# Three 16-bit products per dense token in the expert layer, narrower 32-bit products, and one set of h rows spread eight blocks later

## The chip, the core and the metric

The kernel runs on one core of one Trainium2 chip. The metric is device microseconds (us) of one execution, lower is better: 2103.4 us is the median of 3 runs, which lie between 2100.66 and 2104.29 us. The trace is of one execution, taken by the hardware profiler. PE is the TensorE matmul, PEld its weight load, DVE the VectorE, ACT the ScalarE, POOL the GpSimd engine, SP the engine that issues the large loads.

## The reference, cut to what matters

Two blocks run on 256 tokens of width 1024. The first has two layers, each with a convolution branch, a causal attention of 8 heads with values of 64 wide, and a gated branch of 4 heads of 64. The second has two mixers and behind each an expert layer, which is where most of the time goes:

```
q = (h @ w_q).reshape(B, S, 8, 2, 128)
scores = einsum('bshpd,hpkd->bshpk', q, sub_keys)        # 2 x 128 keys per head
s1, i1 = top_k(scores[..., 0, :], 16); s2, i2 = top_k(scores[..., 1, :], 16)
cand = s1[..., :, None] + s2[..., None, :]               # 256 sums per head
top_s, top_pos = top_k(cand, 16)
ids  = take(i1 * 128 + i2, top_pos)                      # 16 of 16384 experts
gate = softmax(top_s)
act  = gelu(einsum('thk,td->thk over d', u_tab[ids], h)) # u and v rows of the experts
out  = einsum('thk,thkd->td', gate * act, v_tab[ids])
```

A token has 8 heads x 16 = 128 slots; each slot has a gate and an expert, named by two keys below 128.

## The kernel before, in words

Nearly all data and products are 32-bit. The first layers, the mixers and the head of the expert layer are ordered by a scheduler; the body of the expert layer stands in a block whose order is written by hand (`tc.manual_schedule()`), so that each engine's instructions stand as the loop issues them. Each engine works its own list in that order, and an instruction that waits holds up those behind it.

**The expert layer (`peer`, called twice).** The first TS = 96 tokens are done by gathers: an indirect DMA (`fetch`) brings the u row and later the v row of slot k, one row per partition, and `own(k)` works on it in one DVE instruction (L1323 for u, L1332 for v). Their h rows are needed spread over partitions, 32 tokens at a time: `own_rows(r)` copies columns of hT with ACT (L1294, L1295) into a tile of the 12-deep ring "r", turns them on PE (L1299), and ACT writes them to one half of "hh" (L1300).

The other TD = 160 tokens are dense: the kernel multiplies them with all 16384 experts. In the u stage the loop goes over 128 blocks of 128 experts. In block j `u_mm` (L1353) multiplies a block of u with hT, 8 products of 160 columns, and `u_act` of block j-1 applies gelu on ACT and writes W (L1360, L1363). W[:, j, t] must also be multiplied with the gate of expert and token, zero for nearly all. That is spread in groups g of 4 tokens, one group every second block from j = 40 on, 40 groups:

- `hot(g)`: DVE compares the two keys of each slot with 0..127 (L1370), two one-hot matrices per token; ACT multiplies the second with the gates (L1373, 4 instructions).
- `meet(g)`, two blocks later: PE multiplies the two matrices of each token over the 128 slots (L1380), which gives its 128 x 128 grid of gates.
- `put(g)`, two blocks later again: DVE multiplies the grid into the blocks of W that are done (L1388), ACT copies it into those that aren't (L1390), where `u_act` then multiplies (L1364).

After block 127 the v stage (L1452) multiplies W with v, block by block.

The slots of the second 128 tokens are turned into columns by `slot_columns` at j = 39 (L1184, L1188), with rows that DVE makes at j = 29 and 34 (L1175, L1154). `own_rows(1)` stands at j = 37, `own_rows(2)` at j = 72. The ring "r" holds the gathered rows, the one-hot matrices and the tiles of `own_rows`.

**The first layers.** Sums of squares come from products with a matrix of ones, 128 columns of which one is read (L510). In `values` each head's product with v (L726 to L728) takes the v of two neighbouring heads, 128 columns, and half of the result is used; in `sgu` (L822) it is the same with the gated rows.

Of the kernel before, what the change touches and what calls it, by code (L numbers as in the profile page):

```python
# [137 lines left out]
class Kernel:  # L138
# [322 lines left out]
    def first_layer(self, l):  # L461
        nc, tc = self.nc, self.tc
        W = lambda u: self.w3(f"win{l}", u * SLOT)
        with tc.tile_pool(name=f"l{l}", bufs=1) as pl, tc.tile_pool(name=f"m{l}", bufs=2) as pm:
# [9 lines left out]
            with tc.tile_pool(name=f"a{l}", bufs=1) as pa:  # L474
# [17 lines left out]
                for g in range(4):  # L492
                    if g == 1:
                        with self.behind():
                            w = W(g)
                    else:
                        w = W(g) if g else first
                    ps = self.proj3_T(w)
                    self.ada(ADA[l][0][g])
                    sq = self.t(pm, (P, 2, S), "sq")  # L500
                    nc.scalar.activation(sq, ps, AF.Square)
                    for a in range(2):
                        f = 2 * g + a
                        gain = self.col("q_norm_g", f, l) if f < 6 else self.col("kv_norm_g", f - 6, l)
                        if a:
                            nc.vector.tensor_scalar(cT[:, f], ps[:, a], gain, None, op0=ALU.mult)
                        else:
                            nc.scalar.activation(cT[:, f], ps[:, a], AF.Copy, scale=gain)
                        for b in range(2):
                            nc.tensor.matmul(pss[:, (0 if f < 6 else 2) + b], sq[:, a, b * P:(b + 1) * P],  # L510
                                             self.ones[:, :P], start=f == 0 and b == 0, stop=f == 7 and b == 1,
                                             skip_group_check=True)
# [198 lines left out]
    def values(self, pm, sc, rl, v, y):  # L711
        nc = self.nc

        po = [[self.acc.tile([P, 4, P], F32, name="acc") for _ in range(2)] for _ in range(2)]
        for h in range(8):
# [8 lines left out]
            vv = [v[:, b, h - h % 2:h - h % 2 + 2].rearrange("p a d -> p (a d)") for b in range(2)]  # L724
            o = [po[b][h // 4][:, h % 4] for b in range(2)]
# [3 lines left out]
        for b in range(2):  # L729
            yv = y[:, b, 256:768].rearrange("p (h d) -> p h d", h=8)  # L730
            for g in range(2):
                for e in range(2):
                    hs = slice(4 * g + e, 4 * g + 4, 2)
                    nc.vector.tensor_tensor(yv[:, hs], po[b][g][:, e::2, e * 64:(e + 1) * 64],
                                            rl[:, hs, b:b + 1].to_broadcast([P, 2, 64]), op=ALU.mult)
# [59 lines left out]
    def sgu(self, l, pl, pm, wm, wuv):  # L795
# [22 lines left out]
        def mix(y):  # L818
            for b in range(2):
                ps = self.psum((P, 4, P))  # L820
                for h in range(4):
                    nc.tensor.matmul(ps[:, h], ws[:, h], gs[b][:, (h // 2) * P:(h // 2 + 1) * P], start=True, stop=True)  # L822
                for h in range(4):
                    nc.vector.scalar_tensor_tensor(y[:, b, 768 + h * 64:768 + (h + 1) * 64],
                                                   ps[:, h, (h % 2) * 64:(h % 2 + 1) * 64],
# [366 lines left out]
    def peer(self, l):  # L1192
# [9 lines left out]
        with ExitStack() as ctx:  # L1202
# [63 lines left out]
            accs = [lr[:, k * D:(k + 1) * D] for k in (1, 0)]  # L1266

# [67 lines left out]
            with tc.manual_schedule():  # L1335
# [30 lines left out]

                def hot(g):
                    o = self.rp.tile([P, 2, 4, P], F32, name="r")
                    k = TS + 4 * g
                    nc.vector.tensor_tensor(o, self.iota[:, None, None].to_broadcast([P, 2, 4, P]),  # L1370
                                            slots[:, 1:3, k:k + 4, None].to_broadcast([P, 2, 4, P]), op=ALU.is_equal)
                    for t in range(4):
                        nc.scalar.activation(o[:, 1, t], o[:, 1, t], AF.Copy, scale=slots[:, 0, k + t:k + t + 1])  # L1373
                    one[g] = o

                def meet(g):
                    o = one.pop(g)
                    ps = self.acc.tile([P, 4, P], F32, name="acc")
                    for t in range(4):
                        nc.tensor.matmul(ps[:, t], o[:, 0, t], o[:, 1, t], start=True, stop=True)  # L1380
# [16 lines left out]
                for j in range(P):  # L1397
# [21 lines left out]
                    if j == 39:  # L1419
                        self.slot_columns(1, *late, slots)  # L1420
                        c1.close()
                        wts["b"] = self.t(pool("pw"), (P, P - JW, TD), "Wb")
                    if j in (37, 72):
                        own_rows(1 if j == 37 else 2)
# [105 lines left out]
```

## Time and profile before

| | |
|---|---|
| median of 3 runs | 2103.4 us (2100.66 to 2104.29) |
| profiled execution: its own time, its span in the trace | 2102.61 us, 2100.9 us |
| u stage of the expert layer, first and second (window) | 661 to 996, 1469 to 1804 us |
| v stage, first and second (window) | 996 to 1285, 1804 to 2088 us |
| TensorE granted clock, mean | 0.979 of full speed |

The time is 1.7 us above the span; the rest of the text counts in the span and adds that. A matmul in 32 bits leaves two records per product in the trace, one in 16 bits leaves one, and a record's duration is longer than the distance to the next, since they are pipelined: what one costs is read from the distance between starts of runs of them. The same holds for DVE and ACT in short: an instruction of 1.22 us can be followed 1.14 us after its start. An idle time that the profile shows in brackets ends with the engine named behind the arrow.

### The profile page before, as it was taken

The page shows a single profiled execution, that of the slowest core. Times are in us where ns is not written, and L with a number is a line of the kernel's source. Part 1 is how long each engine was busy: PE and PEld are TensorE (multiplying, and loading weights), DVE is VectorE, ACT ScalarE, POOL GpSimd, SP SyncE. Part 2 cuts the span into 40 slices and gives each one's busy share as a digit, 9 for nine tenths or more (in the row PEclk, how much of TensorE's full clock was granted, in tenths as well). Part 3 has the DMA queues.
Part 4 walks back from the last instruction along what each step waited for, and adds up shares of the span by engine and source line. Part 5 has one row for each costly group of instructions (what it writes and reads, how often), then busy time and mean ns, then how long its engine had stood idle before and what let it go on. Part 6 is the DMA issues. An engine that isn't in the chain of part 4 may idle for free. (4 is left out here: it accounts for less than half of the span.)

```text
span 2100.9 us, 35398 instructions
## 1 busy us (share of the span) xinstructions
PE 1998.1 (95%) x13860; PEld 1871.6 (89%) x13860; DVE 1403.3 (67%) x3068; ACT 617.7 (29%) x1684; POOL 626.3 (30%) x683
## 2 busy tenths in 40 slices
PE   6997998999999989999999998999989999999997
PEld 6683795888769989999999998969989999999997
DVE  7698588577657777788444446976796788544344
ACT  4452472455433134433000002743224433000000
POOL 0201111011001564443343440001374444243442
PEclk9998999999999999999999998999999999999999
DMA  9647738442414999999999998643799999999996
GB/s 343 233 160 265 262 111 310 149 123 71 161 61 157 356 405 364 358 365 363 381 415 416 415 415 338 243 180 120 294 404 377 353 366 372 356 416 416 415 415 270
DMA packets 123719, 630.01 MB, mean 300 GB/s; under 512 B 13728, under 2 KB 14368, under 8 KB 79264
## 3 DMA queue, kind: packets, MB, share of 16 engines
q1 hardware_dynamic: 66960, 422.87, 52.5%
q0 software_dynamic: 55296, 201.35, 24.6%
q10 hardware_dynamic: 1296, 3.53, 0.5%
q8 instruction: 109, 1.79, 0.3%
q14 instruction: 58, 0.48, 0.1%
HBM read 626.65 MB, written 1.05 MB: 299 GB/s over the span
## 5 line engine op out<-in xcount | busy, mean ns | idle before, releaser
L1353 PE MATMUL ps<-hT,w 128*128 128x160 f32 x4096 | 574.8, 300 | 0.0
L1353 PEld LDWEIGHTS ps<-hT,w 128*128 128x128 f32 x4096 | 562.4, 191 | 0.0
L1332 DVE SCALAR_TENSOR_TENSOR hl<-r,asl,hl 128x1024 f32<-128x1024 f32 x186 | 239.0, 1285 | 314.8 <-DMA r<-v,ids 314.2
L1452 PE MATMUL acc<-Wa,w 128*128 128x160 f32 x2560 | 348.4, 299 | 0.0
L1452 PEld LDWEIGHTS acc<-Wa,w 128*128 128x128 f32 x2560 | 347.9, 190 | 0.0
L1311 POOL DMA_INDIRECT r<-v,ids x192 | 232.0, 1208 | 346.4 <-PE acc L1452 255.1
L1311 POOL DMA_INDIRECT r<-urow,ids x192 | 252.7, 1316 | 243.3 <-DVE r L1323 133.6
L1323 DVE SCALAR_TENSOR_TENSOR r<-r,hh 128x1024 f32<-128x1024 f32 x192 | 231.9, 1218 | 2.2 <-DMA r<-urow,ids 1.9
L1452 PE MATMUL acc<-Wb,w 128*128 128x160 f32 x1536 | 209.6, 299 | 0.2 <-DMA w<-v 0.2
L1452 PEld LDWEIGHTS acc<-Wb,w 128*128 128x128 f32 x1536 | 208.8, 190 | 0.5 <-DMA w<-v 0.5
L1471 ACT ACTIVATE hT<-acc,mod 128x256 f32<-128x256 f32 x8 | 3.7, 475 | 569.6 <-DVE hT L1473 569.6
L1373 ACT ACTIVATE r<-r,hl 128x128 f32<-128x128 f32 x320 | 102.3, 391 | 233.7 <-DVE r L1370 233.7
L257 PE MATMUL ps<-hh,r 128*128 128x256 f32 (+1 forms) x464 | 135.9, 293 | 4.6 <-ACT r L229 2.9
L259 PE MATMUL ps<-hh,r 128*128 128x256 f32 (+1 forms) x464 | 133.6, 288 | 6.6 <-DVE r L230 6.6
L258 PE MATMUL ps<-hl,r 128*128 128x256 f32 (+1 forms) x464 | 133.7, 288 | 1.0 <-DVE hl L381 1.0
L270 DVE SCALAR_TENSOR_TENSOR w<-w,crow 128x1024 f32<-128x1024 f32 x96 | 113.6, 1216 | 3.2 <-ACT crow L835 3.2
L230 DVE TENSOR_TENSOR r<-w,r 128x1024 fp32r<-128x1024 f32 (+1 forms) x82 | 97.5, 1199 | 27.2 <-ACT r L229 26.2
L229 ACT ACTIVATE r<-w 128x1024 fp32r<-128x1024 f32 (+1 forms) x82 | 84.3, 1039 | 77.8 <-PE ps L258 34.3
L1370 DVE TENSOR_TENSOR r<-cst,hl 128x1024 f32<-128x1024 f32 x80 | 97.4, 1218 | 0.0
L259 PEld LDWEIGHTS ps<-hh,r 128*128 128x128 f32 (+1 forms) x464 | 89.0, 192 | 7.9 <-DVE r L230 7.6
L257 PEld LDWEIGHTS ps<-hh,r 128*128 128x128 f32 (+1 forms) x464 | 89.5, 193 | 6.2 <-ACT r L229 3.8
L258 PEld LDWEIGHTS ps<-hl,r 128*128 128x128 f32 (+1 forms) x464 | 89.3, 193 | 2.1 <-DVE hl L381 1.6
(382 smaller groups left out, 2910.0 us busy)
## 6 DMA issues: line engine op xcount, KB each, us to landing
w<-u SPq DMA_DIRECT2D x128, 1024.0 KB, 8.0
w<-v SPq DMA_DIRECT2D x128, 1024.0 KB, 8.3
w<-ada SPq DMA_DIRECT2D x48, 1024.0 KB, 4.9
w<-win SPq DMA_DIRECT2D x24, 1024.0 KB, 5.0
r<-hgin SPq DMA_DIRECT2D x40, 512.0 KB, 4.4
w<-wq SPq DMA_DIRECT2D x12, 1024.0 KB, 5.0
r<-wout SPq DMA_DIRECT2D x16, 512.0 KB, 8.6
r<-wmid SPq DMA_DIRECT2D x12, 384.0 KB, 7.6
```

The costliest lines, as they stand in the source:

```text
L230: self.nc.vector.tensor_tensor(lo, x, hi.bitcast(F32), op=ALU.subtract)
L257: mm(ps, a[0], b[0], start=start, stop=False)
L258: mm(ps, a[0], b[1], start=False, stop=False)
L259: mm(ps, a[1], b[0], start=False, stop=stop)
L270: nc.vector.scalar_tensor_tensor(x, x, 1.0, self.cond, op0=ALU.mult, op1=ALU.mult, accum_out=m[:, j + i:j + i + 1])
L1311: g = nc.gpsimd.indirect_dma_start(out=x, out_offset=None, in_=A[f"urow{l}"] if k < TS else vrow, in_offset=at)
L1323: nc.vector.scalar_tensor_tensor(x, x, 1.0, hrep[r % 2], op0=ALU.mult, op1=ALU.mult, accum_out=asl[:, g:g + 1])
L1332: nc.vector.scalar_tensor_tensor(accs[r % 2], x, asl[:, g:g + 1], accs[r % 2], op0=ALU.mult, op1=ALU.add)
L1353: nc.tensor.matmul(ps, u[:, c], hT[:, c, TS:], start=c == 0, stop=c == 7)
L1370: nc.vector.tensor_tensor(o, self.iota[:, None, None].to_broadcast([P, 2, 4, P]), slots[:, 1:3, k:k + 4, None].to_broadcast([P, 2, 4, P]), ...
L1373: nc.scalar.activation(o[:, 1, t], o[:, 1, t], AF.Copy, scale=slots[:, 0, k + t:k + t + 1])
L1452: mm = nc.tensor.matmul(acc[c // 2][:, c % 2, TS:], v[:, c * P:(c + 1) * P], W(j), start=j == 0 and c % 2 == 0, stop=False, skip_group_che ...
```

## The change

Four edits.

- `own_rows(1)` moves from j = 37 to j = 45.
- The products with ones have 32 columns, those of `values` and `sgu` 64 instead of 128. The eight DVE multiplications behind `values` become four of twice the size.
- `gate_parts`, new at j = 39 behind `slot_columns`: DVE splits the 160 dense tokens' gates into three 16-bit parts whose sum is the gate, in 8 instructions.
- `hot` makes its one-hot matrices in 16 bits, in planes 0 and 3 of a tile of four. ACT writes plane 1 and 2, plane 3 times the first and the second part, 8 instructions per group; then DVE multiplies plane 3 in place with the third part. `meet` makes three 16-bit products per token, added up in PSUM.

```
-                            nc.tensor.matmul(pss[:, (0 if f < 6 else 2) + b], sq[:, a, b * P:(b + 1) * P],
-                                             self.ones[:, :P], start=f == 0 and b == 0, stop=f == 7 and b == 1,
+                            nc.tensor.matmul(pss[:, (0 if f < 6 else 2) + b, :32], sq[:, a, b * P:(b + 1) * P],
+                                             self.ones[:, :32], start=f == 0 and b == 0, stop=f == 7 and b == 1,
...
-            vv = [v[:, b, h - h % 2:h - h % 2 + 2].rearrange("p a d -> p (a d)") for b in range(2)]
-            o = [po[b][h // 4][:, h % 4] for b in range(2)]
+            vv = [v[:, b, h] for b in range(2)]
+            o = [po[b][h // 4][:, h % 4, :64] for b in range(2)]
...
-                    nc.tensor.matmul(ps[:, h], ws[:, h], gs[b][:, (h // 2) * P:(h // 2 + 1) * P], start=True, stop=True)
+                    nc.tensor.matmul(ps[:, h, :64], ws[:, h], gs[b][:, h * 64:(h + 1) * 64], start=True, stop=True)
...
+                def gate_parts():
+
+                    rest, half = slots[:, 0, TS:], self.t(pl, (P, TD), "half", BF16)
+                    for i in range(3):
+                        nc.vector.tensor_copy(half, rest)
+                        nc.vector.tensor_copy(gp[:, i], half)
+                        if i < 2:
+                            nc.vector.tensor_tensor(gp[:, 2], rest, gp[:, i], op=ALU.subtract)
+                            rest = gp[:, 2]
+
                 def hot(g):
-                    o = self.rp.tile([P, 2, 4, P], F32, name="r")
+
+                    o = self.rp.tile([P, 4, 4, P], BF16, name="r")
                     k = TS + 4 * g
-                    nc.vector.tensor_tensor(o, self.iota[:, None, None].to_broadcast([P, 2, 4, P]),
+                    nc.vector.tensor_tensor(o[:, 0::3], self.iota[:, None, None].to_broadcast([P, 2, 4, P]),
                                             slots[:, 1:3, k:k + 4, None].to_broadcast([P, 2, 4, P]), op=ALU.is_equal)
+                    k = 4 * g
                     for t in range(4):
-                        nc.scalar.activation(o[:, 1, t], o[:, 1, t], AF.Copy, scale=slots[:, 0, k + t:k + t + 1])
+                        for i in range(2):
+                            nc.scalar.activation(o[:, 1 + i, t], o[:, 3, t], AF.Copy, scale=gp[:, i, k + t:k + t + 1])
+                    nc.vector.tensor_tensor(o[:, 3], o[:, 3], gp[:, 2, k:k + 4, None].to_broadcast([P, 4, P]), op=ALU.mult)
                     one[g] = o
 
                 def meet(g):
                     o = one.pop(g)
                     ps = self.acc.tile([P, 4, P], F32, name="acc")
                     for t in range(4):
-                        nc.tensor.matmul(ps[:, t], o[:, 0, t], o[:, 1, t], start=True, stop=True)
+                        for i in range(3):
+                            nc.tensor.matmul(ps[:, t], o[:, 0, t], o[:, 1 + i, t], start=i == 0, stop=i == 2)
                     two[g] = ps
...
+                        gate_parts()
                         wts["b"] = self.t(pool("pw"), (P, P - JW, TD), "Wb")
-                    if j in (37, 72):
-                        own_rows(1 if j == 37 else 2)
+                    if j in (45, 72):
+                        own_rows(1 if j == 45 else 2)
```

In what the diff makes of each engine's list two places matter. The first is DVE in the first u stage, from one comparison of `hot` (g = 3) to the next (in brackets the semaphores that an instruction waits for, by the engine that raises them). Before:

```order
L1370 TENSOR_TENSOR r<-cst,hl 128x1024 [waits DVE_49]
L1388 TENSOR_TENSOR Wa<-Wa,acc 128x4x46 [waits PE_49]
L1364 TENSOR_TENSOR Wa<-Wa,act 128x8 [waits Activation_49]
L1323 SCALAR_TENSOR_TENSOR r,asl<-r,hh 128x1024 [waits DMASW5_49]
L1364 TENSOR_TENSOR Wa<-Wa,act 128x8 [waits Activation_49]
L1323 SCALAR_TENSOR_TENSOR r,asl<-r,hh 128x1024 [waits DMASW6_49]
L1370 TENSOR_TENSOR r<-cst,hl 128x1024 [waits DVE_49]
```

The same stretch of DVE's list now, where L1380 is the comparison, L1386 the new multiplication with the third part, L1402 the multiplication of `put`, L1363 that of `u_act` and L1322 `own`:

```order
L1380 TENSOR_TENSOR r<-cst,hl 128x2x512
L1386 TENSOR_TENSOR r<-r,hl 128x512 [waits DVE_49,Activation_49]
L1402 TENSOR_TENSOR Wa<-Wa,acc 128x4x46 [waits PE_49]
L1363 TENSOR_TENSOR Wa<-Wa,act 128x8 [waits Activation_49]
L1322 SCALAR_TENSOR_TENSOR r,asl<-r,hh 128x1024 [waits DMASW5_49]
L1363 TENSOR_TENSOR Wa<-Wa,act 128x8 [waits Activation_49]
L1322 SCALAR_TENSOR_TENSOR r,asl<-r,hh 128x1024 [waits DMASW6_49]
L1380 TENSOR_TENSOR r<-cst,hl 128x2x512 [waits PE_49]
```

One instruction has come in, directly behind the comparison, and it waits for ACT.

The second is ACT over the same group. Before (L1373 multiplies with the gates, L1390 is the copy of `put`, L1360 and L1363 the gelus of `u_act`):

```order
L1373 ACTIVATE r<-r,hl 128x128 [waits DVE_49]
L1373 ACTIVATE r<-r,hl 128x128 x3
L1390 ACTIVATE Wa<-acc 128x4x34 [waits DVE_49]
L1390 ACTIVATE Wb<-acc 128x4x48
L1360 ACTIVATE Wa<-ps 128x152 [waits PE_49]
L1363 ACTIVATE act<-ps 128x8
```

The same stretch of ACT's list now (L1385 multiplies with the first two parts, L1404 is the copy of `put`, L1359 and L1362 the gelus):

```order
L1385 ACTIVATE r<-r,hl 128x128 [waits DVE_49]
L1385 ACTIVATE r<-r,hl 128x128 x7
L1404 ACTIVATE Wa<-acc 128x4x34 [waits DVE_49]
L1404 ACTIVATE Wb<-acc 128x4x48
L1359 ACTIVATE Wa<-ps 128x152 [waits PE_49]
L1362 ACTIVATE act<-ps 128x8
```

Four multiplications have become eight; the copies and gelus stand behind them as before.

## Rows read from the trace of the kernel before

**Rows 1.** The page's first part: busy us, share of the span, instructions.
```profile
PE 1998.1 (95%) x13860; PEld 1871.6 (89%) x13860; DVE 1403.3 (67%) x3068; ACT 617.7 (29%) x1684; POOL 626.3 (30%) x683
```
**Rows 2.** Waits of PE over the whole span: us in total, times, longest.
```profile
PE ps L1299 <- ACT r L1295: 20.1, 4, 8.7
```
**Rows 3.** A 16 us window: PE, PEld, DVE, ACT, POOL, clock, DMA share, GB/s.
```profile
1549.00:1565.00 16.00, 7.33 (x53) 7.09 (x52) 15.08 (x48) 3.54 (x7) 12.14 (x14) 0.82 0.99 386
```
**Rows 4.** PE in order of time: start, us, what, [idle before it].
```profile
1564.30 1.97 PE L1299 MATMUL ps<-cst,r 128*128 128x128 f32 x8 [8.67 <-ACT r L1295]
...
1572.24 1.95 PE L1188 MATMUL ps<-identh,r 128*128 128x128 bf16 x32
1574.03 6.74 PE L1353 MATMUL ps<-hT,w 128*128 128x160 f32 x48
...
1585.84 1.05 PE L1380 MATMUL acc<-r 128*128 128x128 f32 x8
1586.73 4.51 PE L1353 MATMUL ps<-hT,w 128*128 128x160 f32 x32
1591.08 1.05 PE L1380 MATMUL acc<-r 128*128 128x128 f32 x8
...
1789.37 15.38 PE L1353 MATMUL ps<-hT,w 128*128 128x160 f32 x112
1804.58 1.66 PE L1452 MATMUL acc<-Wa,w 128*128 128x160 f32 x11
```
**Rows 5.** DVE in order of time, the first groups of the second u stage.
```profile
1564.13 0.28 DVE L1152 TENSOR_REDUCE wsm<-wk 128x8 f32<-128x128 f32 x1
...
1564.88 1.22 DVE L1323 SCALAR_TENSOR_TENSOR r<-r,hh 128x1024 f32<-128x1024 f32 x1
...
1571.81 1.21 DVE L1370 TENSOR_TENSOR r<-cst,hl 128x1024 f32<-128x1024 f32 x1
...
1590.73 1.22 DVE L1370 TENSOR_TENSOR r<-cst,hl 128x1024 f32<-128x1024 f32 x1
1591.87 0.50 DVE L1388 TENSOR_TENSOR Wa<-Wa,acc 128x184 f32<-128x184 f32 x1
1594.11 0.17 DVE L1364 TENSOR_TENSOR Wa<-Wa,act 128x8 f32<-128x8 f32 x1 [1.74 <-ACT act L1363]
...
1596.56 1.22 DVE L1370 TENSOR_TENSOR r<-cst,hl 128x1024 f32<-128x1024 f32 x1
```
**Rows 6.** DVE in order of time, the last two groups.
```profile
1780.81 1.22 DVE L1370 TENSOR_TENSOR r<-cst,hl 128x1024 f32<-128x1024 f32 x1
1781.95 0.78 DVE L1388 TENSOR_TENSOR Wa<-Wa,acc 128x320 f32<-128x320 f32 x1
1782.62 0.45 DVE L1388 TENSOR_TENSOR Wb<-Wb,acc 128x144 f32<-128x144 f32 x1
1783.72 0.31 DVE L1364 TENSOR_TENSOR Wb<-Wb,act 128x148 f32<-128x148 f32 x1 [0.65 <-ACT act L1363]
...
1786.46 1.22 DVE L1370 TENSOR_TENSOR r<-cst,hl 128x1024 f32<-128x1024 f32 x1
```
**Rows 7.** ACT in order of time, beside the groups of rows 5 and 6.
```profile
1593.17 0.39 ACT L1390 ACTIVATE Wa<-acc 128x136 f32<-128x136 f32 x1
...
1782.06 1.28 ACT L1373 ACTIVATE r<-r,hl 128x128 f32<-128x128 f32 x4 [3.76 <-DVE r L1370]
1783.25 0.23 ACT L1390 ACTIVATE Wb<-acc 128x48 f32<-128x48 f32 x1
```
**Rows 8.** Groups by line and form: count, busy us, mean ns, idle before.
```profile
L944 DVE TENSOR_TENSOR r<-hbE 128x512 f32<-128x512 f32 x28 | 19.1, 681 | 0.0
...
L568 ACT ACTIVATE junk<-y 128x512 bf16<-128x512 f32 x2 | 1.3, 632 | 2.5 <-DVE y L565 2.5
L564 ACT ACTIVATE z<-z 128x512 f32<-128x512 f32 x2 | 1.3, 626 | 0.0
```
**Rows 9.** The chain that ended last: start, us, what.
```profile
1909.07 1.76 PE acc L1446 x16
```

More of the change, by code (lines that the diff above doesn't have):

```diff
@@ L731, in values @@
             for g in range(2):
[L732 to L735, printed above, removed]
+                hs = slice(4 * g, 4 * g + 4)
+                nc.vector.tensor_tensor(yv[:, hs], po[b][g][:, :, :64], rl[:, hs, b:b + 1].to_broadcast([P, 4, 64]),
+                                        op=ALU.mult)
     def conv(self, l, pl, yp):
@@ L821, in mix @@
                 for h in range(4):
-                    nc.tensor.matmul(ps[:, h], ws[:, h], gs[b][:, (h // 2) * P:(h // 2 + 1) * P], start=True, stop=True)
+                    nc.tensor.matmul(ps[:, h, :64], ws[:, h], gs[b][:, h * 64:(h + 1) * 64], start=True, stop=True)
                 for h in range(4):
                     nc.vector.scalar_tensor_tensor(y[:, b, 768 + h * 64:768 + (h + 1) * 64],
-                                                   ps[:, h, (h % 2) * 64:(h % 2 + 1) * 64],
+                                                   ps[:, h, :64],
                                                    self.col("sg_b", h, l), us[b][:, h * 64:(h + 1) * 64],
@@ L1266, in peer @@
             accs = [lr[:, k * D:(k + 1) * D] for k in (1, 0)]
+            gp = lr[:, D:D + 3 * TD].rearrange("p (k t) -> p k t", k=3)
             def own_slots():
```

## The prediction

> **What bounds the kernel now.** I read the page's first part, then PE's waits, then 16 us windows of the expert layer's u stages, and in them PE, DVE and ACT in order of time. The first part [rows 1] says PE 95% busy, DVE 67%: a kernel bound by PE, it seems. The reader is to see that this average doesn't hold for the place of the change. In a u stage a group of 4 dense tokens costs PE 0.89 us for `meet` (8 records, 1585.84 to 1586.73) and 4.35 us for two blocks of u (1586.73 to 1591.08), 5.24 us together [rows 4]. DVE needs about as long: from the first comparison of `hot` (1571.81) to that of group 39 (1786.46) it takes 214.65 us, 39 rounds of 5.50 us [rows 5, 6]. A round with two gathered rows takes 5.83 us early (1590.73 to 1596.56) and 5.65 us at the end (1780.81 to 1786.46). So two chains run side by side at nearly one pace, and which of them an edit burdens decides. I follow the second u stage; the first has the same length (both fill a window of 335 us).
>
> **The change part by part.**
>
> *Three 16-bit products on PE.* Now 8 records take 0.89 us. The only 16-bit products of this size are those of `slot_columns`: 32 in 1.79 us (1572.24 to 1574.03), 0.056 us each with their weight loads [rows 4]. Twelve cost 0.67 us, so PE gains 0.22 us per group, 17.6 us over 80 groups, if PE sets the pace. The Trainium skill ("TensorE: Matmul & The Clock Gate", section "Back-to-back issue gap") states about 81 ns per product of 128 columns in a stream with weight loads; by that twelve would cost 0.97 us, and the edit would lose 6.6 us on PE. The trace has 56 ns, so I go by it; the sentence matters only for the rival in which PE decides.
>
> *Eight instead of four multiplications on ACT, and one more on DVE.* This is the part that decides. In DVE's list the new multiplication stands directly behind the comparison, and it overwrites the plane that ACT's eight instructions read. DVE works in order, so it stands still until ACT has done the eighth. Queued behind it are `put`, `u_act`'s multiplication and the gathered rows, and PE waits for that multiplication too (`meet`), and through ACT's gelus for free PSUM tiles.
>
> How long DVE stands still: ACT starts 1.25 us after the comparison started (1780.81 to 1782.06), and its next instruction comes 1.19 us later, 0.297 us for each of the four [rows 6, 7]. The four last 1.28 us, eight last 1.28 + 1.19 = 2.47 us. So DVE's next instruction starts 1.25 + 2.47 = 3.72 us after the comparison, instead of 1.14 us (1590.73 to 1591.87): **+2.58 us**. That 16 bits make ACT no faster is in the trace: 512 columns took 632 ns into 16 bits and 626 ns into 32 [rows 8]. The bounds of one multiplication are two copies of `put` on ACT: 0.23 us (48 columns, as if 128 in 16 bits took no more) and 0.39 us (136 columns, without overlap) [rows 7]; I take 0.297, the same instruction.
>
> The multiplication itself: 128x512 lasts 0.68 us [rows 8], and a DVE instruction is followed 0.08 us before its recorded end (1.22 and 1.14 us): **+0.60 us**. No row shows one on 16 bits; the bounds are 0.34 us (half of the 0.68) and 1.14 us (a whole comparison).
>
> What DVE gets back: it now waits for ACT behind `put`, 1.74 us early and 0.65 us late [rows 5, 6]. Part stays, since ACT's copies of `put` wait for DVE's `put` in its list: from the first of them to DVE's next instruction it is 0.94 us early (1593.17 to 1594.11) and 0.47 us late (1783.25 to 1783.72) [rows 5 to 7]. So 0.79 us come back early and, with a hand-over, 0.15 us late.
>
> A round with two gathered rows is then 5.83 + 2.58 + 0.60 - 0.79 = 8.22 us early and 5.65 + 2.58 + 0.60 - 0.15 = 8.68 us late. 96 rows on 112 blocks are 1.71 per group, and one row is 1.14 us; 0.29 x 1.14 = 0.33 us off gives 7.89 and 8.35, **8.12 us** in the mean. PE's 5.02 us fit in, so PE waits and its gain is lost.
>
> The 39 rounds: the first two have no `put` yet, 3.72 + 0.60 + 1.14 = 5.46 and with two rows 6.60 us; 37 x 8.12 = 300.4 us; 4 us for the two times that `own_rows` now takes ACT's time inside this loop. Together 316.5 us for 214.65 us: **+101.9 us per stage**.
>
> *`gate_parts`.* Eight small instructions ahead of the first comparison, each behind the one before. Three such took 0.75 us (1564.13 to 1564.88) [rows 5]: **+2.0 us per stage**, in DVE's list, which is full there (15.08 of 16 us [rows 3]). Bounds 0 and 4 us.
>
> *The end of the stage.* From the last comparison to the v stage it was 1804.58 - 1786.46 = 18.1 us. Now 3.72 + 0.60 us, 0.67 us of `meet`, and the seven blocks behind it, 15.2 us (1789.37 to 1804.58) [rows 4, 6], 20.2 us: **+2.1 us per stage**.
>
> *Rows of h later.* PE stood 20.1 us at the transposes of `own_rows`, in four waits [rows 2]; the one at j = 37 was 8.67 us, and at a clock granted at 0.82 of full speed in that window [rows 3] the eight records and two blocks behind it took 7.94 us (1564.30 to 1572.24) where 0.89 + 4.35 = 5.24 us would do [rows 4]. With PE as the bound, taking this out is worth 8.67 + 2.7 = 11 us per stage. But those waits end with DVE's gathered rows, which hold tiles of the ring, and DVE's own list up to the first comparison doesn't get shorter: `slot_columns` at j = 39 then waits for the slots' weights (done at 1564.88 [rows 5]) in its place. With DVE setting the pace I count 0. At j = 45 the copies wait for a tile in a loop that PE waits in anyway.
>
> *Narrower products.* Does the time of a 32-bit product fall with its columns? The narrowest in the trace, 96 columns, took 1.76 us for 16 records, 0.110 us each [rows 9]; with 128 columns it is 0.89 / 8 = 0.111 us [rows 4]. It doesn't; I count 0. In proportion to the columns, 64 records of L510, 96 of `values` and 32 of `sgu` would save 64 x 0.083 + 128 x 0.056 = 12.5 us, the other end, if nothing else held those places. The Trainium skill has both answers in that same page: by "Step-by-step: what each phase is for" the time is that of the N columns fed in, which gives up to these 12.5 us; by "LDWEIGHTS (loading the stationary operand)" a load of 128 columns takes 128 / 1.2 = 107 ns whatever follows, which gives 0. The rows side with the second. Fewer DVE instructions behind `values` and the order that a scheduler moves in the first layers: 0, with 5 us either way.
>
> **Sum.** 101.9 + 2.0 + 2.1 = 106 us per stage, 212 us for both. The profiled execution took 2102.6 us (1.7 above its span), 0.8 us under the median; 2102.6 + 212 gives 2315 us.
>
> **The rivals.**
>
> *PE stays the bound: faster.* If DVE's wait for ACT were covered, the 17.6 us of `meet` and 2 x 11 us of `own_rows` would go: 2102.6 - 40 = 2063 us. (By the skill's 81 ns it would be 2087 us.) For it: PE's 95%. Against: DVE's rounds at 5.50 us already exceed PE's 5.24 us [rows 4 to 6], and the new instruction has nothing between itself and what it waits for. It holds if a DVE round stays under 5.02 us. Chance 0.05.
>
> *Only DVE's work counts, not its wait.* Then a round grows by 0.60 us: 39 x 0.60 + 4 us per stage, 55 us for both, 2158 us. It would need ACT to be done early, by eight instructions of hardly any length. Chance 0.05.
>
> *PE falls to half clock.* In each round PE now has a gap of 8.12 - 5.02 = 3.1 us. After the gap at 1564 its records went at half speed for some us [rows 4]. If the lower level (1.2 GHz) were granted throughout, PE would need 2 x 5.02 = 10.0 us per group and be the bound again: 37 x 1.9 us more per stage, 2456 us. Against: at that level PE has no gap left, and 8.67 us of idle brought it down for no longer than a few us. Chance 0.04.
>
> *The change doesn't do what it says.* The later `own_rows` may give nothing and the narrower products nothing; that is within my forecast, since I count both at 0.
>
> **How the numbers follow.** The forecast gets 0.86: 2315 us. Its own range: the multiplication between 0.34 and 1.14 us is -20 to +43 us over 78 rounds, but one so far off the 0.60 is unlikely, and I take half of each; an ACT instruction between 0.23 and 0.39 us (eight of them, 78 rounds) is -42 to +58 us, and of that I take a third, since it is the same instruction; what DVE gets back may be off by 0.3 us, 23 us either way; -12 us for the narrow products; some us of half clock at the end of each stage. Added as independent, some 45 to 50 us: 2268 to 2370 us. With 0.04 above it and 0.10 below, the whole leaves no more than 2 in 10 out. A measurement of this kernel tells 0.2% (4 us) from no change. Faster 0.05 (the first rival), same 0.01, slower 0.94.
>
> **What would show it.** In the profile after: DVE idle 2.5 us in front of L1386, released by ACT L1385, in nearly all of 80 groups; rounds of 8 us between comparisons; PE waiting in L1394 for DVE, some 3 us per group, and busy well under 80% in the u stages; the u stages about 440 us instead of 335; v stages as before; L1394's products 0.056 us apart; `values` and L510 at 0.11 us per record as before. A DVE wait in front of L1386 of under 0.5 us, or comparisons 5 us apart, would prove the main step wrong.

## The result: 10.8% slower

The changed kernel takes 2330.5 us (median of 6 runs, 2324.4 to 2333.4) where the kernel before takes 2103.9 us (median of 6 runs). The ratio is 1.1076, with a 95% interval from 1.1058 to 1.1095. 2315 us was predicted, in a range of 2268 to 2370 us.

The profiled execution has a span of 2327.9 us, 227.0 us more than before. By stretches, in us:

| | before | after | difference |
|---|---|---|---|
| start to the first u stage | 661.8 | 677.2 | +15.4 |
| first u stage (first L1352 to first product of v) | 334.4 | 442.9 | +108.5 |
| second u stage | 335.2 | 444.0 | +108.8 |
| first v stage and the layer up to the second u stage | 473.2 | 467.5 | -5.8 |
| second v stage to the end | 296.3 | 296.3 | 0 |

### The profile page after: what moved, and what is told of

It is laid out like the page before. It is cut to its first block, busy times and chain, and to the rows that moved or that the text cites. A ratio compares the mean times of both kernels' runs of the same rounds, so it can differ in the third digit from the quotient of the medians.

```text
span 2327.9 us, 36531 instructions
## 1 busy us (share of the span) xinstructions
PE 2072.6 (89%) x14180; PEld 1929.6 (83%) x14180; DVE 1460.7 (63%) x3156; ACT 719.1 (31%) x2004; POOL 626.7 (27%) x683
## 3 DMA queue, kind: packets, MB, share of 16 engines
q0 software_dynamic: 55296, 201.35, 23.3%
## 5 line engine op out<-in xcount | busy, mean ns | idle before, releaser
L1352 PE MATMUL ps<-hT,w 128*128 128x160 f32 x4096 | 628.2, 317 | 2.0 <-issue 2.0
L1352 PEld LDWEIGHTS ps<-hT,w 128*128 128x128 f32 x4096 | 612.2, 205 | 2.4 <-issue 2.3
L1385 ACT ACTIVATE r<-r,hl 128x128 bf16<-128x128 bf16 x640 | 195.5, 387 | 259.6 <-DVE r L1380 259.6
L1322 DVE SCALAR_TENSOR_TENSOR r<-r,hh 128x1024 f32<-128x1024 f32 x192 | 231.7, 1219 | 1.4 <-DMA r<-urow,ids 1.4
L1394 PE MATMUL acc<-r 128*128 128x128 bf16 x960 | 90.6, 234 | 143.8 <-DVE r L1386 127.0
L1394 PEld LDWEIGHTS <-r 128*128 128x128 bf16 x960 | 70.8, 104 | 161.7 <-issue 149.6
L1386 DVE TENSOR_TENSOR r<-r,hl 128x512 bf16<-128x512 bf16 x80 | 55.4, 692 | 201.1 <-ACT r L1385 201.1
L1380 DVE TENSOR_TENSOR r<-cst,hl 128x1024 bf16<-128x1024 f32 x80 | 97.6, 1220 | 0.0
```

The source lines that it names most:

```text
L1322: nc.vector.scalar_tensor_tensor(x, x, 1.0, hrep[r % 2], op0=ALU.mult, op1=ALU.mult, accum_out=asl[:, g:g + 1])
L1352: nc.tensor.matmul(ps, u[:, c], hT[:, c, TS:], start=c == 0, stop=c == 7)
L1380: nc.vector.tensor_tensor(o[:, 0::3], self.iota[:, None, None].to_broadcast([P, 2, 4, P]), slots[:, 1:3, k:k + 4, None].to_broadcast([P, 2 ...
L1385: nc.scalar.activation(o[:, 1 + i, t], o[:, 3, t], AF.Copy, scale=gp[:, i, k + t:k + t + 1])
L1394: nc.tensor.matmul(ps[:, t], o[:, 0, t], o[:, 1 + i, t], start=i == 0, stop=i == 2)
```

## The profile after

Names of lines after: L1380 is the comparison, L1385 ACT's multiplications, L1386 the new multiplication on DVE, L1394 the products of `meet`, L1402 and L1404 `put` on DVE and on ACT, L1352 u's products, L1359 and L1362 the gelus, L1363 `u_act` on DVE, L1322 the gathered rows.

The page's first part (busy us, share of the span, instructions):

```profile
PE 2072.6 (89%) x14180; PEld 1929.6 (83%) x14180; DVE 1460.7 (63%) x3156; ACT 719.1 (31%) x2004; POOL 626.7 (27%) x683
```

Against [rows 1] the shares of PE, DVE and POOL have fallen, and ACT's has risen only from 29 to 31%. No engine has become the bound: they wait for each other. Who for whom stands in the waits of DVE and of PE (us in total, times, longest):

```profile
DVE r L1386 <- ACT r L1385: 201.1, 80, 2.6
DVE Wa L1363 <- ACT act L1362: 36.6, 37, 2.6
DVE Wb L1363 <- ACT act L1362: 29.1, 43, 1.8
```
```profile
PE acc L1394 <- DVE r L1386: 127.0, 68, 2.3
PE ps L1298 <- ACT r L1294: 19.3, 4, 4.9
PE acc L1394 <- ACT r L1385: 14.5, 24, 1.3
...
PE ps L1182 <- DVE wk L1152: 6.7, 2, 3.4
```

201.1 us in 80 waits are 2.51 us in front of every one of the 80 new multiplications, and behind DVE it is PE that waits, 127 + 14.5 us in all, 1.8 us per group. Its wait for the rows of h is about as long as in [rows 2], now inside the loop.

DVE in order of time, a round early and one at the end of the second u stage (start, us, what, [idle before it]); it answers to [rows 5, 6]:

```profile
1715.98 1.22 DVE L1380 TENSOR_TENSOR r<-cst,hl 128x1024 bf16<-128x1024 f32 x1
1719.71 0.69 DVE L1386 TENSOR_TENSOR r<-r,hl 128x512 bf16<-128x512 bf16 x1 [2.51 <-ACT r L1385]
1720.32 0.51 DVE L1402 TENSOR_TENSOR Wa<-Wa,acc 128x184 f32<-128x184 f32 x1
1721.82 0.17 DVE L1363 TENSOR_TENSOR Wa<-Wa,act 128x8 f32<-128x8 f32 x1 [1.00 <-ACT act L1362]
...
1724.27 1.22 DVE L1380 TENSOR_TENSOR r<-cst,hl 128x1024 bf16<-128x1024 f32 x1
...
1993.85 1.22 DVE L1380 TENSOR_TENSOR r<-cst,hl 128x1024 bf16<-128x1024 f32 x1
...
1999.82 0.31 DVE L1363 TENSOR_TENSOR Wb<-Wb,act 128x144 f32<-128x144 f32 x1 [0.54 <-ACT act L1362]
...
2002.55 1.22 DVE L1380 TENSOR_TENSOR r<-cst,hl 128x1024 bf16<-128x1024 f32 x1
```

From the comparison to the new multiplication 3.73 us; the multiplication 0.61 us to the next start; a wait for the gelus behind `put` of 1.00 us early and 0.54 us late; rounds of 8.29 and 8.70 us. Over the stage, 39 rounds take 318.5 us (1692.75 to 2011.26), 8.17 us in the mean, where they took 214.65 us.

ACT and PE beside that early round (rows of before: [rows 7] and [rows 4]):

```profile
1717.23 2.44 ACT L1385 ACTIVATE r<-r,hl 128x128 bf16<-128x128 bf16 x8 [2.51 <-DVE r L1380]
```
```profile
1716.39 0.83 PE L1394 MATMUL acc<-r 128*128 128x128 bf16 x12
1717.06 4.57 PE L1352 MATMUL ps<-hT,w 128*128 128x160 f32 x32
...
1728.81 0.72 PE L1394 MATMUL acc<-r 128*128 128x128 bf16 x10 [2.01 <-DVE r L1386]
```

ACT's eight last 2.44 us: that is the wait. Twelve products take 0.67 us of PE (1716.39 to 1717.06), as forecast, less than the eight records before; and then PE stands 2 us in front of most of them. What that did to its clock stands in the windows of the 39 rounds (length; busy us of PE, PEld, DVE, ACT, POOL; clock; DMA share, GB/s). Before, in the first and the second u stage:

```profile
764.51:978.05 213.54, 211.99 (x1627) 211.66 (x1625) 163.03 (x307) 84.34 (x371) 97.58 (x70) 1.00 0.98 368
1571.81:1786.46 214.65, 213.11 (x1642) 212.81 (x1641) 163.08 (x307) 84.32 (x371) 98.55 (x71) 1.00 0.97 368
```

and after:

```profile
781.38:1099.81 318.43, 239.19 (x1728) 229.93 (x1727) 189.24 (x346) 135.67 (x529) 97.37 (x70) 0.89 0.71 250
1692.75:2011.26 318.51, 238.18 (x1721) 228.93 (x1720) 189.31 (x346) 135.69 (x529) 96.18 (x70) 0.89 0.71 249
```

The granted clock fell from 1.00 to 0.89, in stretches at the lower of its two levels (1.2 GHz). The rounds hardly show it, since PE's longer work falls into its wait for DVE: in the second stage a round with two rows takes 8.56 us where part of it is at the lower level (19 rounds) and 8.46 us where none is (9).

The same windows show what a round is made of. DVE was busy for 163.08 of 214.65 us before and for 189.31 of 318.51 us after: 4.18 and 4.85 us a round. It stood still for 1.32 us of a round before and for 3.31 us after. So its own work grew by 0.67 us a round and its waiting by 1.99 us.

## The experiments

Before the runs the theory was: the cost is DVE's standing still for ACT's eight, in an instruction right behind the comparison. The rivals: the number of instructions, on DVE or on ACT; the later rows of h; something in the narrower products, since the first layers had become 15 us longer.

**Each part alone.** e1_narrow is the kernel before with the narrower products, e2_rows with `own_rows(1)` at 45, e3_gates with the three 16-bit products; each takes its lines of the diff shown above, nothing else.

> The kernel before with the narrower products alone (32 columns with ones, 64 in values and sgu). In the changed kernel's trace the second u stage of the expert layer's first call begins at 677.1 us instead of 661.6 us, and around its narrow products (140 to 160 us) the granted clock is 0.57 with PE busy 18.9 of 20 us. Theory: these products alone cause that, the records come no closer together and the clock is granted at its lower level beside them: 2103.9 + 15 = 2119 us, u stage from 677 us on, clock about 0.6 in values. Rival, the prediction's own count: 0, 2104 us, the 15 us come from something else. Second rival, time by columns: 12 us less, 2091 us.

Measured: 2111.7 us (6 runs) against 2101.3, ratio 1.0054 [1.0034, 1.0073], 10.4 us more (7 to 15), where the theory said 15. The parts that run wholly outside the u stages do cost, and both other answers (nothing, or a gain in proportion to the columns) fall.

> The kernel before with own_rows(1) at j = 45 alone. Theory: DVE's list sets when the first comparison of hot comes (1571.8 us in the second u stage) and its 39 rounds of 5.5 us set the end, so PE's wait of 8.7 us only moves, to slot_columns and meet: 2104 us, within 4 us. Rival, PE is the bound: two waits of 8.7 us and 2.7 us of low clock each go, 2081 us.

Measured: 2098.2 us (12 runs), ratio 0.999 [0.9976, 1.0004]: no change that can be told. PE's waits for the rows of h (L1299) shrink from 20.1 to 3.4 us, and a wait for `slot_columns` (L1184) takes part of their place:

```profile
PE ps L1184 <- DVE wk L1154: 9.9, 2, 5.1
PE ps L1299 <- ACT r L1295: 3.4, 2, 1.7
```

In the profiled execution the u stages are 2.0 and 3.4 us shorter than before (332.4 and 331.8 us), too little for the total to tell.

> The kernel before with the three 16-bit products alone (gate_parts, hot, meet). Theory: DVE stands still 2.5 us per group in front of the new multiplication, rounds of 8.17 us instead of 5.5 us; all of the slowdown but the 15 us of the first layers: 2330.5 - 15 = 2315 us. Rival, it takes the three edits together (the move of own_rows puts its ACT work into the loop): 10 us or more below that, under 2305 us.

Measured: 2331.1 us (4 runs), ratio 1.1094 [1.1066, 1.1122], +229.8 us: this edit alone is as dear as the whole change. Its u stages last 447 us, 4 more than with all four edits, while its rounds are no longer (8.10 us). With the rows of h still at block 37, PE's wait for them (L1300 here) is there again,

```profile
PE ps L1300 <- ACT r L1296: 26.5, 4, 8.6
```

and the first comparison comes 109.3 us into the stage instead of 104.2. So the later rows give back about 4 us a stage once the gates are in, and by themselves no more than the 2 to 3 us above.

**The same instructions in another order.** e4_order is the changed kernel with DVE's multiplication one block later (`third`), and in odd blocks the gathered row (`step`, the lines of `own` and `fetch`) ahead of `u_act`:

```
-                    nc.vector.tensor_tensor(o[:, 3], o[:, 3], gp[:, 2, k:k + 4, None].to_broadcast([P, 4, P]), op=ALU.mult)
                     one[g] = o
...
+                    odd = j > G0 and bool((j - G0) & 1)
+                    if odd:
+                        step(j)
+                        if (j - G0) // 2 < NG:
+                            third((j - G0) // 2)
                     if j:
                         u_act(j - 1)
```

> The changed kernel with the same instructions, two of them moved in the loop: the multiplication with the third part is issued one block later, and in that block the gathered row (own) comes ahead of it and of u_act. Theory, the wait is what costs: from the comparison DVE has put and a gathered row to do until ACT's eight are through at 3.72 us; a round with two gathered rows is 3.72 + 0.60 + 0.3 + 0.2 + 1.14, about 5.9 us, 5.6 us in the mean, 217 us for 39 instead of 318.5 us: 2330 - 2 x 101 = 2128 us, L1386's wait below 0.5 us. Rival, the added work itself costs (eight ACT instructions, the multiplication, twelve products): no change beyond 10 us, 2325 us.

Measured: 2149.2 us (4 runs), ratio 1.0228 [1.0202, 1.0253]. Some 180 of the 227 us are gone with not one instruction taken out; the rounds are 5.80 us. That the wait sat where it sat is the main cause, and this shows it. The wait is not wholly gone, and the time lies 21 us above the 2128 forecast. In front of the multiplication (L1390 here) DVE still waits 0.87 us each time, where under 0.5 was expected:

```profile
DVE r L1390 <- ACT r L1385: 67.8, 78, 2.1
```

Of its 80 multiplications 68 have a gathered row ahead of them and wait 0.68 us in the mean; the 12 without one wait 1.78 us. One with a row:

```profile
1640.05 1.22 DVE L1322 SCALAR_TENSOR_TENSOR r<-r,hh 128x1024 f32<-128x1024 f32 x1
...
1642.19 0.69 DVE L1390 TENSOR_TENSOR r<-r,hl 128x512 bf16<-128x512 bf16 x1 [0.92 <-ACT r L1385]
```

So `put` and one row don't cover ACT's eight.

**Without the instruction that waits.** e5_two is the changed kernel without DVE's multiplication and without the third product of each token; it leaves out the gates' third part.

```
-                    nc.vector.tensor_tensor(o[:, 3], o[:, 3], gp[:, 2, k:k + 4, None].to_broadcast([P, 4, P]), op=ALU.mult)
...
-                        for i in range(3):
+                        for i in range(2):
```

> The changed kernel with two 16-bit parts only: the multiplication of plane 3 by DVE and the third product of every token are left out, and with them the gates' third part. ACT's eight multiplications stay. Theory (DVE's standing still for ACT and the multiplication that waits are the cost): without the instruction that waits DVE goes on to the product into W 1.14 us after its comparison. What is left is ACT's four more instructions ahead of its gelus, for which DVE waits later in the round, behind put: 4 x 0.297 = 1.2 us on a round that took 5.50 us before, so 6.6 us, 39 rounds of 257 us instead of 318.5, about 2206 us in all. Rival (ACT's eight instructions by themselves are the cost, wherever DVE stands): rounds stay near 8.17 less the multiplication's 0.60, that is 7.6 us, and the time is about 2285 us. Second rival (the wait alone, ACT's number is free): rounds of 5.5 us, about 2118 us with the 10 us of the narrower products.

Measured: 2200.3 us (4 runs), ratio 1.0461 [1.0436, 1.0486]; rounds of 6.51 us where the theory said 6.6, and 7.6 or 5.5 the rivals. So of the 2.66 us that a round got longer, 1.66 go with the multiplication and its wait, and 1.0 is ACT's four more instructions, for which DVE then waits at its next meeting with ACT, the gelus (L1401 is `put` here):

```profile
1726.22 1.22 DVE L1380 TENSOR_TENSOR r<-cst,hl 128x1024 bf16<-128x1024 f32 x1
1727.36 0.69 DVE L1401 TENSOR_TENSOR Wa<-Wa,acc 128x280 f32<-128x280 f32 x1
1730.57 0.22 DVE L1363 TENSOR_TENSOR Wa<-Wa,act 128x56 f32<-128x56 f32 x1 [2.52 <-ACT act L1362]
```

**A version meant to beat both, and its failure.** e6_act12 gives all three parts to ACT, in the odd block behind `u_act`; DVE has no multiplication left. Without the narrower products, rows of h at 45.

```
+                def spread(g):
+                    o, k = one[g], 4 * g
+                    for t in range(4):
+                        for i in (0, 1, 2):
+                            nc.scalar.activation(o[:, 1 + i, t], o[:, 3, t], AF.Copy, scale=gp[:, i, k + t:k + t + 1])
...
                     if j:
                         u_act(j - 1)
+                    if odd and (j - G0) // 2 < NG:
+                        spread((j - G0) // 2)
```

> The kernel before with the three 16-bit products, made in another way: ACT multiplies with all three parts, twelve instructions per group, one block after the comparison and behind the gelus of that block; DVE has no multiplication, and in odd blocks the gathered row stands ahead of the wait for the gelus. The rows of h are spread at block 45 as in the change; the first layers keep their 128 columns. Theory: nothing in DVE's list waits for these twelve, so DVE's round is its own work, some 4.7 us; ACT's is 12 x 0.297 + about 1.3 us for gelus and copies = 4.8 us; PE needs 0.67 + 4.35 = 5.02 us and sets the pace again. 39 rounds of 5.05 us are 197 us per stage instead of 215, with 2 us for the split of the gates and 2 us at the end: 2 x 14 us off, about 2075 us (2065 to 2095). Rival: ACT with 4.8 us has too little to spare, its gelus come late and PE waits for PSUM tiles: rounds of 5.5 us or more, 2105 us or more.

Measured: 2328.1 us (5 runs), ratio 1.1075 [1.1051, 1.1098], as slow as the change, with rounds of 8.11 us. I had added up each engine's work (4.7, 4.8, 5.0 us) and not followed the lap, the way through both engines' lists from one wait to the next and back. ACT and DVE in order of time (here L1390 is ACT's multiplications, L1364 a gelu, L1365 `u_act` on DVE, L1324 the gathered row, L1405 and L1407 `put` on DVE and on ACT):

```profile
1907.69 4.17 ACT L1390 ACTIVATE r<-r,hl 128x128 bf16<-128x128 bf16 x12
...
1911.86 0.25 ACT L1364 ACTIVATE act<-ps 128x104 f32<-128x104 f32 x1
...
1912.14 0.27 DVE L1365 TENSOR_TENSOR Wb<-Wb,act 128x104 f32<-128x104 f32 x1 [3.62 <-ACT act L1364]
1912.32 1.22 DVE L1324 SCALAR_TENSOR_TENSOR r<-r,hh 128x1024 f32<-128x1024 f32 x1
...
1915.30 0.27 DVE L1405 TENSOR_TENSOR Wb<-Wb,acc 128x64 f32<-128x64 f32 x1
...
1915.60 0.40 ACT L1407 ACTIVATE Wb<-acc 128x128 f32<-128x128 f32 x1 [3.49 <-DVE Wb L1405]
...
1916.04 2.13 ACT L1390 ACTIVATE r<-r,hl 128x128 bf16<-128x128 bf16 x6
```

DVE stands 3.62 us while ACT multiplies, ACT 3.49 us while DVE does its row, comparison and `put`: each works only while the other waits, 8.35 us a lap (1907.69 to 1916.04).

**The lap opened.** e9_act12_late moves the same twelve into the even block, where DVE's 3.5 us lie, and the products one block on; e10_third_late does the same with the change's own instructions, ACT's eight in the even block and DVE's multiplication in the odd one.

```
-                    if odd and (j - G0) // 2 < NG:
-                        spread((j - G0) // 2)
+                    if j > G0 and not odd and (j - G0) // 2 <= NG:
+                        spread((j - G0) // 2 - 1)
...
-                        for g, f in ((n // 2, hot), (n // 2 - 1, meet), (n // 2 - 2, put)):
-                            if n % 2 == 0 and 0 <= g < NG:
+                        for g, f, r in ((n // 2, hot, 0), ((n - 3) // 2, meet, 1), (n // 2 - 2, put, 0)):
+                            if n % 2 == r and 0 <= g < NG:
```

> ACT's twelve multiplications as in the run before, but in another place: in the even block right behind its gelus, one whole round after their comparison, with the products on PE in the odd block behind it; put stays where it was. In the run before, ACT's twelve stood between the gelus of the odd and of the even block, and a lap went through all of it in a row: twelve multiplications 4.1 us (twelve starts 0.34 us apart), the even block's gelus 0.4 us, then DVE's product, gathered row, comparison and put 3.5 us, the copy of put and the odd block's gelus 0.5 us: 8.5 us, and the rounds took 8.11 us. Theory (the lap of mutual waits was the cost, not the number of instructions): now the twelve run while DVE does its 3.5 us, so a round is 4.1 + 0.4 + 0.5 = 5.0 to 5.2 us, near PE's 5.02 us; 39 rounds 199 us per stage in place of 215, 4 us off that for the split of the gates and the stage's end: 2078 us (2068 to 2100). Rival (twelve instructions on ACT are too many wherever they stand): rounds of 6 us or more, 2140 us or more.

Measured: 2101.4 us (12 runs) against 2102.7, ratio 0.9986 [0.997, 1.0001]: 227 us less than e6_act12, with the same instructions. Rounds of 5.22 and 5.29 us; ACT now has next to no gap, and its twelve last as long as before:

```profile
1737.59 4.18 ACT L1390 ACTIVATE r<-r,hl 128x128 bf16<-128x128 bf16 x12
...
1741.68 0.35 ACT L1407 ACTIVATE Wb<-acc 128x112 f32<-128x112 f32 x1
...
1742.66 4.18 ACT L1390 ACTIVATE r<-r,hl 128x128 bf16<-128x128 bf16 x12
```

The rounds give about 9 us a stage; 4 us more before the first comparison and 4 us more at the end (21.9 instead of 18.1 us) take nearly all of it back. The forecast of 2078 fails by both sizes: 39 rounds take 203 and 206 us instead of 199, and the rest costs 8 us a stage instead of 4. The mechanism holds: the rounds are nowhere near the rival's 6 us in the mean.

The trace also tells why the twelve last longer apiece than the change's eight. From one start to the next it is 0.29 to 0.31 us, as in a run of eight, but 0.42 us or a little more in front of every third, which overwrites plane 3 after the two before it have read it. That one carries a wait for ACT's own semaphore and starts 0.03 us after its predecessor has ended, while the others start before that.

> The instructions of the change (ACT eight, DVE one multiplication per group, three products), with ACT's eight in the even block right behind its gelus, one round after their comparison, DVE's multiplication in the odd block behind the gathered row, the products on PE in that odd block; the rows of h at block 45; the first layers keep their 128 columns. Theory: DVE finds ACT's eight done, no wait is left in front of its multiplication, and DVE's own work sets the round: 4.66 + 0.60 = 5.26 us; 39 rounds 205 us in place of 215, 4 us off that: 2 x 6 us, about 2091 us (2080 to 2106). Rival (a wait of about a hand-over with ACT is left in each round whatever the order, as in the run with the third multiplication one block later): rounds of 5.8 us, 2130 us or more.

Measured: 2109.9 us (12 runs), ratio 1.0035 [1.0018, 1.0051]. The wait in front of DVE's multiplication (L1394 here) is gone:

```profile
1741.08 0.70 DVE L1394 TENSOR_TENSOR r<-r,hl 128x512 bf16<-128x512 bf16 x1
```

Rounds are 5.36 and 5.32 us, no longer than the 5.50 us before: so placed, the change's own instructions cost a round nothing. That the forecast of 5.26 us came so near is luck, for DVE's own work does not set the round. In the second stage DVE is busy for 184.52 of 207.40 us and PE for 196.42:

```profile
1586.06:1793.46 207.40, 196.42 (x1675) 191.95 (x1674) 184.52 (x345) 134.00 (x525) 94.29 (x70) 1.00 0.98 370
```

PE's 5.04 us a round lie nearest. The same 4 + 4 us outside the rounds, where 4 in all were forecast, make the sum slightly more than before and more than the 2080 to 2106 us expected.

**Where the narrower products cost.** e7_values has those of `values` and `sgu` alone, e8_ones those with ones alone.

> The kernel before with the narrower products of the values and of the gated branch only (64 columns in place of 128, and four instructions of DVE in place of eight behind the values). The four narrower edits together cost 10.4 us (7 to 15). Theory (the 192 records of the values in a row bring TensorE's clock down while they run, 0.50 instead of 1.00 granted in the first layer, 11.7 us in place of 7.4): most of it, about +8 us, 2111 us, with the lower clock in that stretch in this run's windows too. Rival (it is the order that the scheduler makes with the products with ones): 0, 2103 us, and a granted clock of 1.00 there.

> The kernel before with 32 columns in place of 128 in the products with ones only. The four narrower edits together cost 10.4 us (7 to 15). Theory: these stand in groups of four records between wide products and bring the clock down less (0.79 granted against 0.89 where they run first): about +3 us, 2106 us. Rival: they are the cause of the whole, +10 us, 2113 us; or, in proportion to their columns, -5 us, 2098 us.

Measured: 2106.3 us (ratio 1.0014 [0.9998, 1.0031]) and 2106.6 us (1.0017 [1.0003, 1.003]), 12 runs each, against 2102.8: some 3 to 4 us each, neither the whole, and the first can't be told from nothing. Together they make about 7 of the 10.4 us, within the noise of both. The profiled executions show more, for they differ in where the first u stage starts: at 661.8 to 667.9 us in the six kernels with neither edit and at 670.0 to 677.2 us in the four with both, 665 and 675 us in the mean. So of the 15.4 us in the table of the result some 9 come from the narrower products, and the rest lies within what executions without them differ by.

In the profiled executions most of it is in `values`, though by the medians the two edits cost about alike. From the first to the last product of `values` (64 to 67 records of PE, not the 192 of the expectation), windows of the kernel before in layer one and two (length; PE, PEld, DVE, ACT, POOL; clock; DMA share, GB/s):

```profile
137.64:145.42 7.78, 7.78 (x67) 7.62 (x68) 7.38 (x21) 1.48 (x3) 0.00 (x0) 1.00 1.01 413
317.48:325.24 7.76, 7.76 (x67) 7.60 (x68) 7.38 (x21) 1.48 (x3) 0.00 (x0) 1.00 1.02 416
```

the same in e7_values:

```profile
140.09:152.23 12.14, 12.14 (x64) 12.14 (x65) 5.17 (x12) 1.48 (x3) 0.00 (x0) 0.56 0.89 361
326.17:339.55 13.38, 13.38 (x64) 13.38 (x65) 5.17 (x12) 1.48 (x3) 0.00 (x0) 0.50 0.80 327
```

and in e1_narrow:

```profile
139.70:152.03 12.33, 12.33 (x64) 12.33 (x65) 5.16 (x12) 1.47 (x3) 0.00 (x0) 0.55 0.87 356
325.95:333.06 7.11, 7.11 (x64) 7.11 (x65) 5.06 (x12) 1.47 (x3) 0.00 (x0) 1.00 1.01 414
```

At full clock the narrow stretch takes 7.11 us, 0.7 less than the wide one. But in nine of the ten such stretches of the five profiled runs with 64 columns the granted clock lies at 0.50 to 0.60, near the lower level of 1.2 GHz, and they last up to 13.4 us; with 128 columns it lies between 0.71 and 1.00 in fourteen stretches of seven runs. The profile shows PE without a gap in either. The two stretches together take 23.3 us in the mean of the four runs with both edits and 17.1 us with neither, 6 of the 9 us. The stretch of the products with ones in layer one gives 1.5 us more (27.0 against 25.5 us; clock 0.81 to 0.87 against 0.87 to 1.00); in layer two it is 21 us in both, at 1.00. It differs between executions: the profiled run of e7_values is the slowest of its twelve (2118.6 us; the fastest 2098.6). That the lower clock comes with the edit to `values` is shown by these counts. The edit also halves the number of DVE's instructions behind the products, which was not tried apart. Why the clock falls, and why not in each execution, stays open.

## Why the prediction was right, step by step

- **What bounds.** Right in that the change is paid in DVE's rounds and not on PE, 95% busy on the page before: PE needs 5.24 us a group, and a round takes 8.17 us. But the 5.50 us before were not DVE's work alone; 1.32 us of them were already DVE's waiting, all of it for ACT. It was a lap of the two engines, and the change made it longer.
- **DVE standing still.** Forecast 3.72 us from the comparison to DVE's next instruction, measured 3.73; ACT's eight 2.47, measured 2.44, so 16 bits made ACT no faster. e4_order shows the place to be the cause. One thing the sum did not say: take the waiting instruction away and 1.0 us of the 2.66 us stays (e5_two), since ACT's four more also stand ahead of the gelus.
- **The multiplication.** Forecast 0.60 us from an instruction on 32 bits, measured 0.61.
- **What DVE gets back.** The wait left behind `put` was put at 0.95 us early and 0.50 us late (1.74 less 0.79, 0.65 less 0.15); measured 1.00 and 0.54.
- **The rounds.** 8.22 and 8.68 us forecast with two rows, 8.29 and 8.70 measured; 39 rounds 316.5 against 318.5. Stage +106, measured +108.5 and +108.8.
- **The products on PE.** 0.056 us each as forecast, and the gain of 0.22 us a group was lost in a wait of 2 us. The signs named for PE were a little off: 1.8 us of waiting per group for the multiplication and ACT's eight instead of some 3 us, and 81% busy in the u stages instead of well under 80%. The lower clock, which the sum left out of the rounds, made its work longer. The 81 ns per product that the Trainium skill gives ("TensorE: Matmul & The Clock Gate", section "Back-to-back issue gap") do not hold here: twelve in 0.67 us.
- **`gate_parts` and the stage's end.** +2.0 and +2.1 forecast; from 1687.22 to 1689.50 the eight instructions took 2.28 us, and from the last comparison to v it is 20.3 us, +2.2.
- **Rows of h later, counted at 0.** Right alone as far as the total can tell (0.999); together with the gates about -4 us a stage, which this step missed. The wait for `slot_columns` took the place of the other only in part: 9.9 us came where 16.7 us went.
- **Narrower products, counted at 0: the term that was mis-sized.** It is +10.4 us (7 to 15). That a product does not get cheaper with its columns was nearly right at full clock (7.11 against 7.77 us for the stretch); that its cost would therefore stay the same was wrong, since the clock fell. The ±5 us I left for it were given to the scheduler's order; they were too little, and in the profiled executions most of the cost comes with the clock of `values`. It makes most of the 15 us by which 2315 falls short; the two stages, 2.5 and 2.8 us longer than forecast, and the stretch between them, 5.8 us shorter, nearly cancel.
- **Rivals.** PE as the bound and DVE's work alone both fall with rounds of 8.17 us. PE at half clock is half right: with a wait of some 2 us in most rounds the granted clock was 0.89 over them, and 32 records of u took 6.17 us at 1697.90, where 4.57 us do. But it was not at half throughout, and PE did not become the bound: it waited in front of its products 92 times for DVE or ACT.
- **Between the stages** the profile after is 5.8 us shorter. e8_ones shows 6.2 us less there, e1_narrow none: this can't be told from what differs between executions.

## What to carry to other kernels

Where two engines hand work to each other in every round, don't compare sums of work: write down the lap, who waits for whom in list order, and add what lies in a row; the same twelve instructions made rounds of 8.11 or 5.25 us by their place and that of the products behind them. An instruction that needs another engine's result belongs a step later than the one that asked for it, with work between, and so does what it holds up in the other's list. And a saving in columns on an engine that is busy anyway can come back as a lower clock: look at the granted clock of the stretch before counting it.

## What the runs showed of the hardware

- TensorE, without a gap in the profile in both cases, was granted 0.50 to 0.60 of full speed in nine of ten stretches of narrow 32-bit products and 0.71 to 1.00 in fourteen with the doubled width.
- With waits of about 2 us in most rounds TensorE was granted 0.89 of full speed over 318 us, where the same rounds without them had 1.00.
- Eight ACT multiplications of 128 columns in a row last 2.44 us, twelve 4.17 us: 0.29 and 0.34 us from one to the next. The difference is in every third of the twelve, which overwrites what the two before it read and starts 0.42 us after the one before.
- DVE's multiplication of 512 columns took 0.69 us with 16 bits in and out (its second operand, a column of gates, stayed in 32), and 0.68 us with 32.
